# The state-space stage of an encoder trunk: centred phase frames, merged products, and GLU units taken forth and back

## The chip, the core and the metric

The kernel runs on one core of a Trainium2 chip, as one launch. The metric is device microseconds of one execution; for the kernel before it is the median of three. A profile is one execution, recorded by the hardware profiler: the span from its first to its last instruction, in us.

Engines: PE is TensorE (matmuls; PEld are its weight loads), DVE is VectorE, ACT is ScalarE, POOL is GpSimd, SP is SyncE, which only issues DMAs here. Each engine works through its own instructions in a fixed order and waits for others by semaphores.

## The reference

The input is 256 frames of 2048 channels. The trunk has two layers, each a mixer and a gated convolutional MLP. The first mixer is the state-space stage (S5), which the change is about:

```python
dt = jnp.exp(log_dt)[:, None]
mag = jnp.exp(dt * a_re)
ab_re, ab_im = mag * jnp.cos(dt * a_im), mag * jnp.sin(dt * a_im)
...
x_re = jnp.einsum('blgp,gnp->blgn', ub, bb_re)      # 128 groups of 16 channels, 64 complex states each
x_im = jnp.einsum('blgp,gnp->blgn', ub, bb_im)
... # h[t] = ab * h[t-1] + x[t], an associative scan over the frames
y = (jnp.einsum('blgn,gpn->blgp', hs_re, c_re) - jnp.einsum('blgn,gpn->blgp', hs_im, c_im) + d_skip * ub)
...
y = jax.nn.gelu(y)
val, gate = jnp.split(y @ w_glu + b_glu, 2, axis=-1)
return val * jax.nn.sigmoid(gate)
```

Behind it come an MLP, a shared key/value projection, an attention layer and a second MLP, all fp32, with RMS norms between them. The change does not touch those.

## The kernel before

All matmuls with large weights split each fp32 operand into a high part, written by ACT (`whi`, `act`: line 77), and a low part, the remainder, written by DVE (`wlo`, `act`: line 78), and add three products.

The state-space stage is the first 230 us or so of the program. The recurrence runs in 32 chunks of 8 frames. The 128 groups are handled in 16 blocks of 8 (`n`, `sb` in the code; `nb` is 16), four blocks to a quarter (`PB` is 4).

Start-up, in the order of the code: the rates `sA`; the reduced angle `r` and its sine and cosine `L[1]`; the squares of the input for the first norm (ACT, L144); the powers of the pole to 8 (L341 to L345); the angle per chunk `th` (L347 to L349); the skip weights `dB` times a mask, so that they stand on the diagonal (L358). `first_norm` forms the mean square with one matmul (L367) and `rs_ms` (L121), has POOL take a power, and `refined` improves it by a Newton step on DVE (L128 to L132). `scale_x` multiplies a quarter of the input by its norm weights on DVE (L377) and by the norm on ACT (L379).

For each quarter `powers` builds the pole's first powers by doubling (DVE L402 to L405) and ACT writes them, with signs, as four factors `zs` (L409 to L412). Then, for each block:
- `product` (L462) multiplies factors by the block's input and output matrices `bc` over 128 x 1024 elements: `e1`, `e2` (inputs to states; from block 1 on their sum is formed by an accumulating DMA on POOL's queue) and `f1`, `f2` (states to outputs).
- `frames` (L419 to L424) makes, for two blocks at a time, 32 phase angles per state (a chunk each), brings them into range with three DVE steps of 512 elements, and takes absolute value, sine and cosine on ACT, giving `si` and `co`.
- `part_k` transposes the input into `U` and forms the short convolution kernel `K`, which goes through DRAM (`kd`) and comes back as the Toeplitz matrix `TP`. `part_e` transposes `e` to `ET` (L526, L529 on PE, L530 on ACT).
- `part_v`, `part_r`: the chunks' inputs to the states `vs` are transposed (L546, L547), turned by the frame (L549 to L551), and scanned with the decay `dc` (L557: `R`). `part_h` swaps real and imaginary halves by a matmul (L562) and turns back (L564 to L571: `H`).
- `part_c` adds up the outputs (L438, L445) into `yg` (L583).
- After four blocks `part_d` takes `gelu` (L598), transposes (L602) and splits the result into the activations of the GLU product (L77, L78 with names `act<-wk`).

The product with `w_glu` goes a quarter `b` of its 2048 rows at a time, in four units (`glu_early`), the first two runs of 512 columns of the value and of the gate half; the other columns come after the stage. Each unit opens two PSUM banks, one for each half of the frames, fills them with 24 matmuls (L258, L259, L261) and `glu_keep` moves them to the result `f`: a copy on ACT for quarter 0 (L283), an addition on DVE after that (L285). A generator, `glu_steps`, puts these between the state-space steps of the blocks that follow.

The order around the change is set by the order of the code, by `behind(ins)`, which lets an instruction be issued only after another, and by a scheduler that places the rest within those rules and the number of buffers of each tile. One line shows how the main loop leads:

```python
lead_e(0)
with behind(env["squared"]):
    rs = refined(*rs)
lead_f(0)
scale_x(rs, 0)
for n in range(nb + 2):
```

Two ACT functions need their table loaded (`ACT_TABLE_LOAD`): sine for the frames, `gelu` for `part_d`.

Of the kernel before, what the change touches and what calls it, by code (L numbers as in the profile page):

```python
# [15 lines left out]
P = 128  # L16
# [28 lines left out]
C_SG, C_NSG, C_TPI, C_FR, C_RS, C_HP, C_MH, C_END = 624, 625, 626, 627, 628, 629, 630, 638  # L45
# [3 lines left out]
def tile_trunk(ctx: ExitStack, tc: tile.TileContext, a: dict):  # L49
# [193 lines left out]
    def sincos(si, co, r, n, scale=1.0):  # L243
        dve.scalar_tensor_tensor(n, r, -1.0, r, op0=ALU.mult, op1=ALU.max)
        act.activation(si, r, AF.Sin, scale=scale)
        return act.activation(co, n, AF.Sin, bias=half_pi, scale=-1.0)
# [21 lines left out]
    def glu_early(f, n, b, half):  # L268
        with behind(env["ets"][0]):
            hk, u = glu_load(n, b, half, home=RAWS[2 * n + half] if b == 3 else None)  # L270
        banks = [accb(), accb()]
        for tb in range(NB):
            for i, (wh, wl) in enumerate(u):
                highs(banks[tb], b, tb, i * hk, wh, wl, i == 0, i == 1)
                yield
        glu_keep(f, n, b, half, banks)

    def glu_keep(f, n, b, half, banks):
        o = half * 1024 + n * 512
        for tb in range(NB):  # L280
            c = f[tb][:, o : o + 512]
            if b == 0:
                act.activation(c, banks[tb], AF.Copy)  # L283
            else:
                dve.tensor_tensor(c, banks[tb], c, op=ALU.add)  # L285


    def s5(f):
        with tc.tile_pool(name="s5", bufs=2) as q1, tc.tile_pool(name="dr", bufs=2, space=bass.MemoryType.DRAM) as dr:
# [23 lines left out]
            stepped = dve.tensor_tensor(bz, sA, dt.unsqueeze(1).to_broadcast([P, 2, P]), op=ALU.mult).ins  # L313
# [4 lines left out]
            r, nn = T(q1, [P, P], F32, "R"), T(q1, [P, P], F32, "w2")  # L318
# [27 lines left out]
            th, tn = flat(t1("th")), T(q1, [P, P], F32, "w1")  # L346
            dve.tensor_scalar(th, r, 8.0 * INV2PI, None, op0=ALU.mult)  # L347
# [10 lines left out]
            dve.tensor_tensor(  # L358
                dB.rearrange("p (g q) -> p g q", q=16),
                dB.rearrange("p (g q) -> p g q", q=16),  # L360
                dmask.unsqueeze(1).to_broadcast([P, 32, 16]),
                op=ALU.mult,
            )
# [22 lines left out]
            def powers(qt):  # L386
# [6 lines left out]
                for k, o, i, m in ((1, 7, 8, 1), (2, 5, 7, 2), (4, 1, 5, 4)):  # L393
# [9 lines left out]
                    dve.tensor_tensor(w, v(i), l(1), op=ALU.mult)  # L403
# [7 lines left out]
                act.activation(zz[:, 3], z[:, 1, 1:9, 0, :], AF.Copy, scale=-1.0)  # L411
                act.activation(zz[:, 0], z[:, 0, 0:8, 1, :], AF.Copy)  # L412
                return zz

            def frames(k):
                ps_ = slice(FR * NP * k, FR * NP * (k + 1))
                m, n = T(q1, [P, FR * NP, 32], F32, "si"), T(q1, [P, FR * NP, 32], F32, "co")
                cv = cst[:, C_CV : C_CV + 32].unsqueeze(1).to_broadcast([P, FR * NP, 32])
                dve.tensor_tensor(m, th[:, ps_].unsqueeze(2).to_broadcast([P, FR * NP, 32]), cv, op=ALU.mult)  # L419
                dve.tensor_scalar(n, m, MAGIC, MAGIC, op0=ALU.add, op1=ALU.subtract)  # L420
                dve.tensor_tensor(m, m, n, op=ALU.subtract)
                act.activation(n, m, AF.Abs)
                act.activation(m, m, AF.Sin, scale=cst[:, C_TPI : C_TPI + 1])
                env["sin"] = act.activation(n, n, AF.Sin, bias=half_pi, scale=-TWO_PI).ins  # L424
                return [z.rearrange("p (k n) c -> k p (n c)", k=FR) for z in (m, n)]
# [31 lines left out]
            def product(tag, bufs, sb, i):  # L457
                h = (sb % PB) * NP
                o = T(q1, [P, NP, 8, 16], F32, tag, bufs)
                zt = zs[sb // PB][:, i, :, h : h + NP].rearrange("p i n -> p n i").unsqueeze(3).to_broadcast([P, NP, 8, 16])  # L460
                bt = bc[sb][:, i].unsqueeze(2).to_broadcast([P, NP, 8, 16])
                env["made"] = dve.tensor_tensor(o, zt, bt, op=ALU.mult).ins  # L462
# [78 lines left out]
            def part_r(sb, vs, si, co):  # L541
# [6 lines left out]
                w1, w2 = T(q1, [P, W], F32, "w1"), T(q1, [P, W], F32, "w2")  # L548
# [743 lines left out]
```

## Time and profile before

| | |
|---|---|
| three runs | 2115.04, 2111.18, 2106.82 us; median 2111.18 |
| profiled execution | 2114.63 us, its span 2112.8 us |
| busy over the span | PE 2048.5 us (97%), DVE 1375.0 (65%), ACT 1088.3 (52%), POOL 32.4 (2%) |
| mean granted TensorE clock | 0.991 |
| first 230 us (busy time by stage) | PE 180.62, DVE 203.13, ACT 140.15, POOL 19.39 us busy; clock 0.93 |
| first GLU matmul | 87.36 us after the start of the span |

How to read it: a share of busy time is an average over stages with different limits. The state-space stage is 11% of the span; the rest of the program follows it with PE busy from end to end. In rows of the trace the fields are engine, line, operation, tile written <- tiles read, shape, and in square brackets the idle time ahead of the instruction and what ended it. `wk` and `acc` are PSUM banks; `raw` is the tile of weights just loaded, and of the input at the start; `w` stands for `w1` and `w2`, `e` for `e1` and `e2`, `f` in L462 for `f1` and `f2`.

### The profile page before, as it was taken

What the parts mean: (1) busy time and instruction counts of PE and PEld (TensorE: products, weight loads), DVE (VectorE), ACT (ScalarE), POOL (GpSimd) and SP (SyncE); (2) the same over time, 40 slices, a digit from 0 to 9 for tenths busy, and PEclk for the clock granted to TensorE, in tenths of its full rate; (3) what the DMA queues carried; (4) which work ended last, traced back from release to release, by engine and by line L of the source; (5) the groups of instructions that cost most, each with busy time, mean ns of one, the idle gap of its engine ahead of it and who ended that gap; (6) DMA issues with size and microseconds to landing.
All of it is one profiled execution on the core that took longest, in us unless ns stands there. A gap on an engine that the chain in (4) does not pass through costs nothing.

```text
span 2112.8 us, 30745 instructions
## 1 busy us (share of the span) xinstructions
PE 2048.5 (97%) x12396; PEld 1755.3 (83%) x12396; DVE 1375.0 (65%) x1935; ACT 1088.3 (52%) x1678; POOL 32.4 (2%) x72
## 2 busy tenths in 40 slices
PE   3799999999999999999999999999999999999998
PEld 3677788888888888888888998898888888888886
DVE  8899776665566566656785666656546655665566
ACT  6666455554555345435554555555445544554453
POOL 1000000000000000000000000000000000000000
PEclk9899999999999999999999999999999999999999
DMA  5677875755665566555454445575555556555642
GB/s 158 194 212 188 261 254 172 250 180 182 200 196 181 183 197 197 179 188 192 139 175 146 128 148 179 165 247 191 179 199 189 190 179 199 189 190 179 199 159 80
DMA packets 291967, 391.62 MB, mean 185 GB/s; under 512 B 10224, under 2 KB 205296, under 8 KB 291312
## 3 DMA queue, kind: packets, MB, share of 16 engines
q1 hardware_dynamic: 285632, 374.71, 53.9%
q0 software_dynamic: 2160, 7.87, 2.1%
q10 hardware_dynamic: 4032, 7.08, 1.0%
q8 instruction: 97, 1.59, 0.3%
q14 instruction: 46, 0.38, 0.1%
HBM read 375.73 MB, written 6.03 MB: 181 GB/s over the span
## 4 chain that ended last, share of the span: by engine, by line
PE 87%; DVE 6%; DMA 2%; ACT 2%; issue 1%; SPq 1%; POOL 0%; ACTq 0%; DVEq 0%; POOLq 0%
PE wk L780 29%; PE wk L782 15%; PE acc L116 9%; PE acc L115 9%; PE acc L114 9%; PE wk L114 2%; PE wk L116 2%; PE wk L115 2%; PE wk L438 1%; PE acc L259 1%; PE acc L261 1%; PE acc L258 1%; DVE wlo L78 1%; ACT junk L144 1%; DVE f L462 1%
## 5 line engine op out<-in xcount | busy, mean ns | idle before, releaser
L78 DVE TENSOR_TENSOR wlo<-raw,whi 128x1024 fp32r<-128x1024 f32 (+1 forms) x590 | 699.5, 1188 | 543.9 <-ACT whi L77 541.0
L77 ACT ACTIVATE whi<-raw 128x1024 fp32r<-128x1024 f32 (+1 forms) x590 | 606.2, 1030 | 659.3 <-PE wk L780 341.9
L780 PE MATMUL wk<-act,whi 128*128 128x512 f32 x2688 | 673.7, 392 | 0.0
L780 PEld LDWEIGHTS wk<-act,whi 128*128 128x128 f32 x2688 | 483.9, 189 | 87.0
L782 PEld LDWEIGHTS wk<-act,wlo 128*128 128x128 f32 x2688 | 366.7, 190 | 26.2
L782 PE MATMUL wk<-act,wlo 128*128 128x256 f32 x2688 | 374.8, 282 | 0.0
L116 PE MATMUL acc<-whi,hl 128*128 128x512 f32 x636 | 249.5, 394 | 0.0
L115 PE MATMUL acc<-wlo,hh 128*128 128x512 f32 x636 | 249.3, 392 | 0.0
L114 PE MATMUL acc<-whi,hh 128*128 128x512 f32 x636 | 246.8, 389 | 0.0
L115 PEld LDWEIGHTS acc<-wlo,hh 128*128 128x128 f32 x636 | 119.4, 188 | 27.6
L114 PEld LDWEIGHTS acc<-whi,hh 128*128 128x128 f32 x636 | 119.4, 188 | 26.7 <-ACT hh L77 0.5
L116 PEld LDWEIGHTS acc<-whi,hl 128*128 128x128 f32 x636 | 119.6, 188 | 24.0
L852 DVE SCALAR_TENSOR_TENSOR cv<-gs,cw,cv 128x255 f32<-128x255 f32 (+1 forms) x168 | 80.9, 482 | 17.2 <-ACT cv L850 14.2
L850 ACT ACTIVATE cv<-gs,cb,cw 128x256 f32<-128x256 f32 x84 | 49.9, 594 | 45.5 <-DVE gs L788 45.5
L258 PE MATMUL acc<-whi,act 128*128 128x512 f32 x156 | 66.1, 424 | 2.1 <-ACT act L77 2.1
L78 DVE TENSOR_TENSOR wlo<-x,whi 128x1024 fp32r<-128x1024 f32 x40 | 48.7, 1222 | 28.7 <-ACT whi L77 28.0
L259 PE MATMUL acc<-whi,act 128*128 128x512 f32 x156 | 63.5, 407 | 2.0 <-DVE act L78 1.9
L77 ACT ACTIVATE whi<-x 128x1024 fp32r<-128x1024 f32 x40 | 42.2, 1061 | 39.6 <-PE wk L780 16.4
L115 PE MATMUL acc<-wlo,act 128*128 128x512 f32 (+1 forms) x152 | 54.8, 361 | 1.0 <-DVE wlo L107 0.9
L114 PE MATMUL acc<-whi,act 128*128 128x512 f32 (+1 forms) x152 | 54.1, 358 | 0.3 <-ACT whi L106 0.3
L116 PE MATMUL acc<-whi,act 128*128 128x512 f32 (+1 forms) x152 | 53.9, 356 | 0.0
L261 PE MATMUL acc<-wlo,act 128*128 128x512 f32 x156 | 50.3, 405 | 0.7 <-DVE wlo L78 0.7
(317 smaller groups left out, 2565.8 us busy)
## 6 DMA issues: line engine op xcount, KB each, us to landing
raw<-in_w_up SPq DMA_DIRECT2D x86, 1024.0 KB
raw<-in_w_gate SPq DMA_DIRECT2D x84, 1024.0 KB
raw<-in_w_down SPq DMA_DIRECT2D x84, 1024.0 KB
raw<-in_w_glu SPq DMA_DIRECT2D x21, 1024.0 KB
x<-in_w_glu SPq DMA_DIRECT2D x11, 1024.0 KB
raw<-in_w_o SPq DMA_DIRECT2D x9, 1024.0 KB
TP<-kd SPq DMA_DIRECT2D x64, 128.0 KB
raw<-in_w_ukv SPq DMA_DIRECT2D x8, 1024.0 KB
```

The costliest lines, as they stand in the source:

```text
L77: act.activation(hi, src, AF.Copy)
L78: (eng or dve).tensor_tensor(lo, src, hi.bitcast(F32), op=ALU.subtract)
L114: pe.matmul(o, lh, rh, start=first, stop=False)
L115: pe.matmul(o, lh, rl, start=False, stop=False)
L116: pe.matmul(o, ll, rh, start=False, stop=last)
L258: pe.matmul(bank, ah, wh[:, k, :], start=first and k == 0, stop=False)
L259: pe.matmul(bank, al, wh[:, k, :], start=False, stop=False)
L261: pe.matmul(bank, acts(tb, 4 * b + j + k)[0], wl[:, k, :], start=False, stop=last and k == hk - 1)
L780: pe.matmul(o, w, pair(kt), start=kt == 0, stop=False)
L782: pe.matmul(o[:, 0, :], w, pair(kt)[:, 0], start=False, stop=kt == KT - 1)
L850: act.activation(cv[:, ft, :], gv[:, ft, :], AF.Identity, scale=cw[:, 2, n : n + 1], bias=cb[:, n : n + 1])
L852: dve.scalar_tensor_tensor(cv[:, ft, sh:], gv[:, ft, : S - sh], cw[:, 2 - sh, n : n + 1], cv[:, ft, sh:], op0=ALU.mult, op1=ALU.add,)
```

## The change

- **Frames.** The reference point of the phase lies in the middle of the 32 chunks, so there are 16 angles (0.5 to 15.5 times the chunk's), and the other half is their mirror: sine with the other sign, cosine the same. The three DVE steps have 256 elements (now L430 to L432). ACT takes one absolute value of 256 and four sines of 256 (L436, L439, L440), two of them written backwards, into one tile `cosi` with cosine and sine side by side. `frames` and `trig` are separate functions. Only frame 0 is asked for in the start-up; the DVE steps are issued behind the last product made.
- **Merged products.** `f` is one product of 2048 elements (now L478). In `part_r` the two products of 256 are one of 512 (L571), into a tile `ww` that replaces `w1` and `w2`. For the first, `zs` is laid out by block: ACT writes runs of 8 with a stride.
- **Skip weights.** `dX` comes laid on the diagonal from the host; the multiply is gone.
- **GLU units.** Quarters 1 and 3 take the four units in reverse, and the last unit of a quarter and the first of the next, which are the same columns, share their PSUM banks. 24 evacuations on DVE become 18, 8 on ACT stay.
- **Splits.** The splits in `part_d` read and write in another order of axes, 128x4x16x4 instead of 128x4x4x16.
- **First steps.** `sA * sA` and the reciprocal are behind the fold of the first angle; `scale_x(rs, 0)` and the Newton step are behind the last pair of products in `powers`; `lead_e(0)` and the first frame come before `lead_f(0)`. The copies of the decay into `dc` are behind the first sine. `part_e(0)` comes before `part_k(0)`, and the first trigonometry behind its evacuation.

The number and kind of TensorE's matmuls are the same; SP and POOL keep their order.

```diff
-    def glu_early(f, n, b, half):
+    def glu_early(f, n, b, half, i):
         with behind(env["ets"][0]):
-            hk, u = glu_load(n, b, half, home=RAWS[2 * n + half] if b == 3 else None)
-        banks = [accb(), accb()]
+            hk, u = glu_load(n, b, half, home=RAWS[i] if b == 3 else None)
+        banks = env["open"] if i == 0 and b else [accb(), accb()]
+        env["open"] = banks
+        begins, ends = i > 0 or b == 0, i < 3 or b == 3
         for tb in range(NB):
-            for i, (wh, wl) in enumerate(u):
-                highs(banks[tb], b, tb, i * hk, wh, wl, i == 0, i == 1)
+            for h, (wh, wl) in enumerate(u):
+                highs(banks[tb], b, tb, h * hk, wh, wl, begins and h == 0, ends and h == 1)
...
-        glu_keep(f, n, b, half, banks)
-
-    def glu_keep(f, n, b, half, banks):
+        if ends:
+            glu_keep(f, n, half, banks)
+
+    def glu_keep(f, n, half, banks):
         o = half * 1024 + n * 512
+        fresh = o not in env["kept"]
+        env["kept"].add(o)
         for tb in range(NB):
             c = f[tb][:, o : o + 512]
-            if b == 0:
+            if fresh:
                 act.activation(c, banks[tb], AF.Copy)
             else:
                 dve.tensor_tensor(c, banks[tb], c, op=ALU.add)
...
+            pr, qr = t1("pu", 2), t1("pw", 2)
+            with behind(env["fold"]):
                 dve.tensor_tensor(pr, sA, sA, op=ALU.mult)
...
-            dmask = cst[:, C_DM : C_DM + 16]
-            dve.tensor_tensor(
-                dB.rearrange("p (g q) -> p g q", q=16),
-                dB.rearrange("p (g q) -> p g q", q=16),
-                dmask.unsqueeze(1).to_broadcast([P, 32, 16]),
-                op=ALU.mult,
-            )
...
-                zz = T(q1, [P, 4, 8, 32], F32, "zs")
-                act.activation(zz[:, 1], z[:, 1, 0:8, 1, :], AF.Copy, scale=cst[:, C_SG : C_SG + 1])
-                act.activation(zz[:, 2], z[:, 0, 1:9, 0, :], AF.Copy, scale=cst[:, C_NSG : C_NSG + 1])
...
+                    dve.tensor_tensor(v(o)[:, 1], u[:, 1], w[:, 0], op=ALU.add)
+                zz = T(q1, [P, PB, 4, NP, 8], F32, "zs")
+
+                def blocks(v):
+                    return v.rearrange("p i (b n) -> p i b n", b=PB)
+
+                def factor(t):
+                    return zz[:, :, t].rearrange("p b n i -> p i b n")
+
+                act.activation(factor(1), blocks(z[:, 1, 0:8, 1, :]), AF.Copy, scale=cst[:, C_SG : C_SG + 1])
+                act.activation(factor(2), blocks(z[:, 0, 1:9, 0, :]), AF.Copy, scale=cst[:, C_NSG : C_NSG + 1])
...
                 return zz
 
             def frames(k):
                 ps_ = slice(FR * NP * k, FR * NP * (k + 1))
-                m, n = T(q1, [P, FR * NP, 32], F32, "si"), T(q1, [P, FR * NP, 32], F32, "co")
-                cv = cst[:, C_CV : C_CV + 32].unsqueeze(1).to_broadcast([P, FR * NP, 32])
-                dve.tensor_tensor(m, th[:, ps_].unsqueeze(2).to_broadcast([P, FR * NP, 32]), cv, op=ALU.mult)
+                z = T(q1, [P, FR, 2, NP, 32], F32, "cosi")
+                shape = [P, FR * NP, 16]
+                m, n = (
+                    flat(T(q1, [P, w, P], F32, t, 1)[:, :2]).rearrange("p (n c) -> p n c", c=16) for t, w in (("sA", 3), ("uu", 2))
+                )
+                cv = cst[:, C_CV : C_CV + 16].unsqueeze(1).to_broadcast(shape)
+                with behind(env["made"]):
+                    dve.tensor_tensor(m, th[:, ps_].unsqueeze(2).to_broadcast(shape), cv, op=ALU.mult)
                 dve.tensor_scalar(n, m, MAGIC, MAGIC, op0=ALU.add, op1=ALU.subtract)
                 dve.tensor_tensor(m, m, n, op=ALU.subtract)
+                return z, m, n
+
+            def trig(z, m, n):
                 act.activation(n, m, AF.Abs)
-                act.activation(m, m, AF.Sin, scale=cst[:, C_TPI : C_TPI + 1])
-                env["sin"] = act.activation(n, n, AF.Sin, bias=half_pi, scale=-TWO_PI).ins
-                return [z.rearrange("p (k n) c -> k p (n c)", k=FR) for z in (m, n)]
+                m4, n4 = (v.rearrange("p (k n) c -> p k n c", k=FR) for v in (m, n))
+                for half, w in ((slice(16, 32), C_TPI), (slice(15, None, -1), C_NTP)):
+                    act.activation(z[:, :, 1, :, half], m4, AF.Sin, scale=cst[:, w : w + 1])
+                    env["sin"] = act.activation(z[:, :, 0, :, half], n4, AF.Sin, bias=half_pi, scale=-TWO_PI).ins
+                return [z[:, k].rearrange("p t n c -> p (t n c)") for k in range(FR)]
...
-            def product(tag, bufs, sb, i):
-                h = (sb % PB) * NP
-                o = T(q1, [P, NP, 8, 16], F32, tag, bufs)
-                zt = zs[sb // PB][:, i, :, h : h + NP].rearrange("p i n -> p n i").unsqueeze(3).to_broadcast([P, NP, 8, 16])
-                bt = bc[sb][:, i].unsqueeze(2).to_broadcast([P, NP, 8, 16])
-                env["made"] = dve.tensor_tensor(o, zt, bt, op=ALU.mult).ins
+            def product(tag, bufs, sb, i, w=1):
+                shape = [P, w * NP, 8, 16]
+                o = T(q1, shape, F32, tag, bufs)
+                zt = zs[sb // PB][:, sb % PB, i : i + w].rearrange("p t n i -> p (t n) i")
+                bt = bc[sb][:, i : i + w].rearrange("p t n q -> p (t n) q")
+                env["made"] = dve.tensor_tensor(
+                    o, zt.unsqueeze(3).to_broadcast(shape), bt.unsqueeze(2).to_broadcast(shape), op=ALU.mult
+                ).ins
...
-                if n % PB == 0:
+                if n % PB == 0 and n:
                     zs[n // PB] = powers(n // PB)
                 e1, e2 = product("e1", 3, n, 0), product("e2", 2, n, 1)
...
-                F[n] = product("f1", 3, n, 2), product("f2", 3, n, 3)
-                if n % FR == 0:
-                    si, co = frames(n // FR)
-                    for k in range(FR):
-                        fr[n + k] = (si[k], co[k])
+                ff = product("f", 3, n, 2, 2)
+                F[n] = ff[:, :NP], ff[:, NP:]
+                if n % FR == 0 and n:
+                    lead_r(n, frames(n // FR))
+
+            def lead_r(n, angles):
+                for k, z in enumerate(trig(*angles)):
+                    fr[n + k] = z
...
-                dve.tensor_tensor(w1, pvt, co, op=ALU.mult)
-                dve.tensor_tensor(w2, pvs, si, op=ALU.mult)
+                ww = T(q1, [P, 2 * W], F32, "ww")
+                w1, w2 = ww[:, :W], ww[:, W:]
+                dve.tensor_tensor(ww, pvv, cs, op=ALU.mult)
...
+                ww = T(q1, [P, 2 * W], F32, "ww")
+                h1, h2 = ww[:, :W], ww[:, W:]
+                dve.tensor_tensor(h1, R, cs[:, :W], op=ALU.mult)
+                dve.tensor_tensor(h2, prs, cs[:, W:], op=ALU.mult)
...
             def glu_steps(b):
-                for n in range(2):
-                    for half in range(2):
-                        yield from glu_early(f, n, b, half)
-                        yield
+                units = [(n, half) for n in range(2) for half in range(2)]
+                for i, (n, half) in enumerate(units[::-1] if b % 2 else units):
+                    yield from glu_early(f, n, b, half, i)
+                    yield
...
-                        return z.rearrange("p j (c t) -> p t j c", t=8)[:, 4 * hh : 4 * hh + 4]
+                        return z.rearrange("p j (c t) -> p j c t", t=8)[:, :, :, 4 * hh : 4 * hh + 4]
 
...
-                        src = ptv.rearrange("p t (j c) -> p t j c", j=4)[:, :, :, 16 * tb : 16 * tb + 16]
+                        src = ptv.rearrange("p t (j c) -> p j c t", j=4)[:, :, 16 * tb : 16 * tb + 16]
                         split(av(hi), av(lo), src)
...
-            lead_e(0)
+            zs[0] = powers(0)
             with behind(env["squared"]):
                 rs = refined(*rs)
+            scale_x(rs, 0)
+            lead_e(0)
+            angles = frames(0)
             lead_f(0)
-            scale_x(rs, 0)
...
         "gX": np.repeat(g("norm_g")[0, 0].reshape(4, 512), 32, 0),
-        "dX": np.repeat(g("ssm_d")[0].reshape(4, 512), 32, 0),
+        "dX": on_diagonal(np.repeat(g("ssm_d")[0].reshape(4, 32, 16), 32, 0)),
```

On DVE in the start-up, from the step after POOL's power to the first products of block 0 (`raw` is the input, `rs` the norm), before:

```order
L128 TENSOR_TENSOR rs_t_245<-rs_y_203 128x8
L420 TENSOR_SCALAR co_440<-si_439 128x512
L402 TENSOR_TENSOR pu_230<-z_213,L_24_129 128x512
L403 TENSOR_TENSOR pw_231<-z_213,L_24_129 128x512
L129 TENSOR_TENSOR rs_t_245<-rs_t_245,rs_ms_201 128x8
L421 TENSOR_TENSOR si_439<-si_439,co_440 128x512
L404 TENSOR_TENSOR z_213<-pu_230,pw_231 128x256
L405 TENSOR_TENSOR z_213<-pu_230,pw_231 128x256
L130 TENSOR_SCALAR rs_t_245<-rs_t_245 128x8
L132 TENSOR_TENSOR rs_r_249<-rs_t_245,rs_y_203 128x8
L462 TENSOR_TENSOR f_73_251<-zs_236,bc_205 128x1024
L462 TENSOR_TENSOR e_69_241<-zs_236,bc_205 128x1024
```

and after:

```order
L128 TENSOR_TENSOR rs_t_238<-rs_y_200 128x8
L378 TENSOR_TENSOR raw_94<-raw_94,gX_104 128x4x128
L405 TENSOR_TENSOR z_210<-pu_227,pw_228 128x256
L406 TENSOR_TENSOR z_210<-pu_227,pw_228 128x256
L129 TENSOR_TENSOR rs_t_238<-rs_t_238,rs_ms_198 128x8
L378 TENSOR_TENSOR raw_95<-raw_95,gX_104 128x4x128
L130 TENSOR_SCALAR rs_t_238<-rs_t_238 128x8
L478 TENSOR_TENSOR e_70_256<-zs_233,bc_202 128x1024
L132 TENSOR_TENSOR rs_r_242<-rs_t_238,rs_y_200 128x8
L478 TENSOR_TENSOR e_69_254<-zs_233,bc_202 128x1024
L430 TENSOR_TENSOR sA_259<-th_176,cst_73 128x256
L478 TENSOR_TENSOR f_264<-zs_233,bc_202 128x2048
```

Ahead of the first product there were two steps of frames (L420, L421, 512 elements each), which are gone from there, and now there are the two `raw` products; the first frame's steps (`sA`, `uu`) stand between products, and `e` comes before `f`.

On ACT at the first `part_d` (`yg` its `gelu`, `act` the splits, `si`, `co` and `cosi` the frame, `whi` a weight split), before:

```order
L598 ACT_TABLE_LOAD
L598 ACTIVATE yg_484<-yg_484 128x512 x2
L77 ACTIVATE whi_1143<-raw_1141 128x1024
L77 ACTIVATE act_212_957<-wk_960 128x4x4x16
L553 ACTIVATE dc_46_186<-mag_19_116 128x8x31
L77 ACTIVATE act_212_957<-wk_969 128x4x4x16
L77 ACTIVATE act_212_957<-wk_960 128x4x4x16
L77 ACTIVATE act_212_957<-wk_969 128x4x4x16
```

and after:

```order
L621 ACT_TABLE_LOAD
L621 ACTIVATE yg_478<-yg_478 128x512 x2
L436 ACTIVATE uu_992<-sA_991 128x256
L439 ACT_TABLE_LOAD
L439 ACTIVATE cosi_990<-sA_991,cst_73 128x2x8x16
L77 ACTIVATE act_198_937<-wk_940 128x4x16x4
L77 ACTIVATE act_198_937<-wk_949 128x4x16x4
L440 ACTIVATE cosi_990<-uu_992,cst_73 128x2x8x16
L439 ACTIVATE cosi_990<-sA_991,cst_73 128x2x8x16
L77 ACTIVATE act_198_937<-wk_940 128x4x16x4
```

The absolute value, the table load for the sine and one sine moved ahead of the first split, and the weight split behind the last.

On ACT at the second `part_d`, before:

```order
L598 ACTIVATE yg_1052<-yg_1052 128x512
L77 ACTIVATE act_348_1639<-wk_1642 128x4x4x16
L422 ACTIVATE co_1696<-si_1695 128x512
L77 ACTIVATE act_348_1639<-wk_1651 128x4x4x16
L423 ACT_TABLE_LOAD
L423 ACTIVATE si_1695<-si_1695,cst_73 128x512
L77 ACTIVATE act_348_1639<-wk_1642 128x4x4x16
L77 ACTIVATE act_348_1639<-wk_1651 128x4x4x16
L424 ACTIVATE co_1696<-co_1696,cst_73 128x512
```

and after:

```order
L621 ACTIVATE yg_1032<-yg_1032 128x512
L77 ACTIVATE act_324_1603<-wk_1606 128x4x16x4
L436 ACTIVATE uu_1656<-sA_1655 128x256
L439 ACT_TABLE_LOAD
L439 ACTIVATE cosi_1654<-sA_1655,cst_73 128x2x8x16
L77 ACTIVATE act_324_1603<-wk_1606 128x4x16x4
L77 ACTIVATE act_324_1603<-wk_1615 128x4x16x4
L440 ACTIVATE cosi_1654<-uu_1656,cst_73 128x2x8x16
L439 ACTIVATE cosi_1654<-sA_1655,cst_73 128x2x8x16
L77 ACTIVATE act_324_1603<-wk_1615 128x4x16x4
L440 ACTIVATE cosi_1654<-uu_1656,cst_73 128x2x8x16
```

The first split keeps its place; the table load, which stood behind the second, now stands ahead of it, and three of the four splits follow the load.

More of the change, by code (lines that the diff above doesn't have):

```diff
@@ L243, in sincos @@
     def sincos(si, co, r, n, scale=1.0):
-        dve.scalar_tensor_tensor(n, r, -1.0, r, op0=ALU.mult, op1=ALU.max)
+        env["fold"] = dve.scalar_tensor_tensor(n, r, -1.0, r, op0=ALU.mult, op1=ALU.max).ins
         act.activation(si, r, AF.Sin, scale=scale)
@@ L317, in s5 @@
             act.activation(mag8, ar, AF.Exp, scale=8.0)
-            r, nn = T(q1, [P, P], F32, "R"), T(q1, [P, P], F32, "w2")
+            r = T(q1, [P, P], F32, "R")
+            ww = T(q1, [P, 4, P], F32, "ww")
+            nn, den, tn = (ww[:, i] for i in range(3))
             reduced(r, phi, nn)
@@ L345, in s5 @@
                 dve.tensor_tensor(L[2 * k][:, 0, :], u[:, 0, :], u[:, 1, :], op=ALU.subtract)
-            th, tn = flat(t1("th")), T(q1, [P, P], F32, "w1")
-            dve.tensor_scalar(th, r, 8.0 * INV2PI, None, op0=ALU.mult)
+            th = flat(t1("th"))
+            with behind(scaled):
+                dve.tensor_scalar(th, r, 8.0 * INV2PI, None, op0=ALU.mult)
             dve.tensor_scalar(tn, th, MAGIC, MAGIC, op0=ALU.add, op1=ALU.subtract)
@@ L373, in scale_x @@
                 c = slice(P * qt, P * qt + P)
-                with behind(env["made"] if qt else None):
+                with behind(env["made"] if qt else env["squared"]):
                     for h in range(2):
@@ L539, in part_v, with part_r @@
                 return vs
-            def part_r(sb, vs, si, co):
+            def part_r(sb, vs, cs):
                 pvv = wk()
@@ L547, in part_r @@
                     pe.transpose(pvs[:, o], vs[:, g, 64:192], ident)
-                w1, w2 = T(q1, [P, W], F32, "w1"), T(q1, [P, W], F32, "w2")
-                dve.tensor_tensor(w1, pvt, co, op=ALU.mult)
-                dve.tensor_tensor(w2, pvs, si, op=ALU.mult)
+                ww = T(q1, [P, 2 * W], F32, "ww")
+                w1, w2 = ww[:, :W], ww[:, W:]
+                dve.tensor_tensor(ww, pvv, cs, op=ALU.mult)
                 dve.tensor_tensor(w1, w1, w2, op=ALU.add)
                 dc = Ds[sb % 2]
-                act.activation(
-                    dc[:, :, 1:32], mag8[:, NP * sb : NP * sb + NP].unsqueeze(2).to_broadcast([P, NP, 31]), AF.Copy
-                )
+                with behind(sine):
+                    act.activation(
+                        dc[:, :, 1:32], mag8[:, NP * sb : NP * sb + NP].unsqueeze(2).to_broadcast([P, NP, 31]), AF.Copy
+                    )
                 R = T(q1, [P, W], F32, "R")
@@ L637, in s5 @@
                 if 0 <= n - 1 < nb:
-                    R = part_r(n - 1, vs, *fr[n - 1])
+                    R = part_r(n - 1, vs, fr[n - 1])
                 if n < nb:
+                    if n == 0:
+                        ET[n] = part_e(E.pop(n))
+                        with behind(env["ets"][-1]):
+                            lead_r(0, angles)
                     U[n], TP[n] = part_k(n, F[n], bc.pop(n))
                     fetch(n + 4, act)
-                    ET[n] = part_e(E.pop(n))
+                    if n:
+                        ET[n] = part_e(E.pop(n))
                 if n > nb:
@@ L1233, in blocks, with on_diagonal @@
         return [np.concatenate([re, im], 1), np.concatenate([im, re], 1)]
+    def on_diagonal(v):
+        out = np.zeros_like(v)
+        for r in range(P):
+            if r % 32 < 16:
+                out[r, :, r % 32] = v[r, :, r % 32]
+        return out.reshape(P, 512)
     pn = lambda v: v.reshape(KT, P).T
```

30 lines of the change are left out of this document (11 added, 19 removed).

## The prediction

> **What bounds the kernel now.** I read the 40 slices of the page first, then busy times by stage, then the waits of the stage that the change touches, and last the timelines at its two narrow places.
>
> ```profile
> PE   3799999999999999999999999999999999999998
> ```
> Each digit is a fortieth of the span (52.8 us). TensorE is short of full in the first two slices alone, so nothing else can give time back, and whatever ends the first stage sooner shifts all the rest.
>
> ```profile
> 25.00:50.00 25.00, 18.39 (x264) 14.40 (x264) 24.62 (x32) 15.85 (x50) 2.77 (x3) 0.93 0.61 137
> 50.00:75.00 25.00, 17.61 (x266) 12.72 (x266) 21.88 (x42) 13.68 (x35) 1.94 (x4) 0.80 0.82 240
> 75.00:100.00 25.00, 20.64 (x241) 16.02 (x242) 22.23 (x40) 15.38 (x30) 1.72 (x2) 0.80 0.57 148
> 100.00:150.00 50.00, 46.78 (x567) 36.93 (x569) 48.17 (x76) 34.70 (x68) 3.65 (x6) 0.97 0.78 214
> 150.00:200.00 50.00, 46.61 (x572) 37.16 (x560) 46.41 (x69) 30.53 (x56) 3.62 (x6) 0.97 0.74 197
> 376.00:2113.00 1737.00, 1724.30 (x9381) 1491.02 (x9380) 1067.66 (x1430) 866.97 (x1252) 9.73 (x25) 1.00 0.55 180
> ```
> The columns are length, then busy us of PE, its weight loads, DVE, ACT and POOL, then the granted TensorE clock. From 25 to 50 us DVE is busy 24.62 of 25 us and PE waits for it; up to 87 us, where the GLU products (`w_glu`) start, DVE stays the pace-maker. Behind 100 us both are nearly full and PE sets the pace; behind 376 us it is PE alone. Vector work taken out before about 87 us moves the end of the program; taken out later it counts only where PE waits for it:
>
> ```profile
> PE wk L367 <- ACT junk L144: 14.3, 1, 14.3
> ...
> PE wk L562 <- DVE R L557: 6.8, 3, 3.0
> PE wk L602 <- ACT yg L598: 3.8, 1, 3.8
> PE wk L562 <- ACT yg L583: 2.2, 1, 2.2
> ...
> PE wk L602 <- ACT yg L598: 2.5, 2, 1.3
> PE acc L258 <- ACT act L77: 1.6, 2, 1.3
> PE acc L259 <- DVE act L78: 1.1, 1, 1.1
> PE wk L562 <- DVE R L557: 1.0, 2, 0.7
> ```
> These are PE's waits (us in all, times, longest): the first row from 0 to 30 us, three from 30 to 95 us, four from 95 to 230 us. Behind 95 us they come to 6.2 us.
>
> **The prices.** From the groups by shape, up to 230 us:
>
> ```profile
> L462 DVE TENSOR_TENSOR f<-zs,bc 128x1024 f32<-128x1024 f32 x32 | 38.8, 1214 | 3.6 <-PE wk L438 3.5
> L285 DVE TENSOR_TENSOR f<-acc,f 128x512 f32<-128x512 f32 x15 | 10.2, 680 | 5.0 <-PE acc L261 5.0
> L549 DVE TENSOR_TENSOR w<-wk,co 128x256 f32<-128x256 f32 x16 | 6.7, 418 | 2.3 <-PE wk L547 2.3
> L419 DVE TENSOR_TENSOR si<-th,cst 128x512 f32<-128x512 f32 x8 | 5.4, 683 | 0.0
> L420 DVE TENSOR_SCALAR co<-si 128x512 f32<-128x512 f32 x8 | 3.3, 414 | 0.0
> ```
> Consecutive instructions overlap, so I price by start to start, in the vector engine's timeline before the first product:
>
> ```profile
> 12.80 0.69 DVE L358 TENSOR_TENSOR dB<-dB,cst 128x512 f32<-128x512 f32 x1 [0.73 <-DMA dB<-in_dX]
> 15.90 0.15 DVE L121 TENSOR_SCALAR rs_ms<-wk 128x8 f32<-128x8 f32 x1
> 16.24 0.68 DVE L377 TENSOR_TENSOR raw<-raw,gX 128x512 f32<-128x512 f32 x1
> 16.84 0.42 DVE L402 TENSOR_TENSOR pu<-z,L 128x256 f32<-128x256 f32 x1
> 17.18 0.42 DVE L403 TENSOR_TENSOR pw<-z,L 128x256 f32<-128x256 f32 x1
> 20.15 0.17 DVE L128 TENSOR_TENSOR rs_t<-rs_y 128x8 f32<-128x8 f32 x1 [1.54 <-POOL rs_y L123]
> 23.63 1.22 DVE L462 TENSOR_TENSOR f<-zs,bc 128x1024 f32<-128x1024 f32 x1
> ```
> A product of 512 costs 0.60 (16.24 to 16.84) and one of 256 costs 0.34: 0.26 for 256 elements and 0.08 fixed. So on DVE:
> - A frame of 256 angles instead of 512 saves 2 x 0.26 + 0.13 (its middle step, L420, lasts as long as a product of 256, so half of it is halved) = 0.65; eight save 5.2. A new frame costs 0.34 + 0.34 + 0.17 = 0.85.
> - Merging two products saves one fixed part: 16 for `f` and 16 in `part_r` x 0.08 = 2.6.
> - Evacuations of GLU banks fall by 6 x 0.60 = 3.6.
> - The multiply of `dB` goes: 0.60.
>
> That is 12.0 us of vector work. [...]
>
> **What of it reaches the end.**
> - Start-up, -2.3. The multiply at 12.80 and a frame's last step, 0.60 each, no longer stand before the mean square at 15.90; the statistics matmul at 14.3 lets that be only 1.0 earlier, so the power on POOL returns at about 19.1 instead of 20.15. From there to the first product the vector engine needed 3.48 us; the new order leaves two products of 512, two of 256 and three small steps ahead of it, 2 x 0.60 + 2 x 0.34 + 0.3 = 2.2. Together 1.0 + 1.3.
> - The stream up to 80 us, +0.3. Frames 0 and 1, which partly stood in that start-up, now run behind the first products (2 x 0.85 = +1.7); frame 2 is cheaper (-0.65); five blocks of merges give -0.8.
> - The first GLU products, 0. The scalar and tensor rows there:
>
> ```profile
> 82.68 1.28 ACT L598 ACT_TABLE_LOAD   x1
> 83.97 1.15 ACT L598 ACTIVATE yg<-yg 128x512 f32<-128x512 f32 x2
> 85.03 1.04 ACT L77 ACTIVATE whi<-raw 128x1024 fp32r<-128x1024 f32 x1
> 85.98 0.61 ACT L77 ACTIVATE act<-wk 128x256 fp32r<-128x256 f32 x1
> 87.36 0.80 PE L258 MATMUL acc<-whi,act 128*128 128x512 f32 x1 [0.48 <-ACT act L77]
> 89.07 0.80 PE L259 MATMUL acc<-whi,act 128*128 128x512 f32 x1
> ```
> Now the fold of a frame (`Abs`), the table load and one sine stand between `gelu` and the first split instead of a 1.0 us weight split: 0.3 + 1.28 + 0.4, about +1.0. Against it the `e` products of block 5 are made earlier, so ACT's evacuations of `ET` ahead of the load should wait less, by about as much.
> - The second and third `part_d`, +1.0. There the load moves ahead of three of the four splits:
>
> ```profile
> 137.44 1.28 ACT L423 ACT_TABLE_LOAD   x1
> 138.73 0.72 ACT L423 ACTIVATE si<-si,cst 128x512 f32<-128x512 f32 x1
> 139.36 1.17 ACT L77 ACTIVATE act<-wk 128x256 fp32r<-128x256 f32 x2
> ...
> 139.48 0.50 PE L259 MATMUL acc<-whi,act 128*128 128x512 f32 x1 [1.15 <-DVE act L78]
> ```
> That delays the second split by 1.28 and half a sine, 1.7. PE has state-space matmuls to put in between: between 0 and 1.7 each, taken as 0.5.
> - Behind 95 us, -2.0. Seven tenths of the vector saving falls here, where PE is the bound, and most is lost. What can go is the 1.0 us for the scan (L562 on R) and most of the 1.1 us for the split, both on a crowded vector engine.
> - ACT, 0. Sixteen more activations, shorter ones. The power factors `zs` and the sines are now written with strides or backwards. Bounds from the shapes at hand:
>
> ```profile
> L77 ACT ACTIVATE act<-wk 128x256 fp32r<-128x256 f32 x14 | 8.5, 656 | 0.6 <-DVE act L78 0.5
> L411 ACT ACTIVATE zs<-z 128x256 f32<-128x256 f32 x4 | 1.6, 409 | 0.0
> ```
> Strided, rounding 256-element splits take 656, contiguous `zs` 409. So at most 0.25 more for each of 16 `zs`, four of them ahead of the first product (up to +1.0); at least nothing, or a few tenths less if the new write pattern of the splits (runs of 4) is quicker. I take zero, nearer the same operation's own row. ACT has 10 us free in each 25, which hides the rest.
> - TensorE, SyncE and POOL keep their instructions; the DMA queues keep their order. Open PSUM banks across units cost nothing while PE's order is unbroken; if another stage wanted these banks, PE itself would wait, at most an evacuation (0.68).
>
> Sum: -2.3 + 0.3 + 0 + 1.0 - 2.0 = -3.0. The profiled execution took 2114.63 us (span 2112.8), 3.45 above the median; it would become 2111.6, the median 2108.2. I forecast **2108**.
>
> **The rivals.** (A) The above.
> (B) *Given back*: the frames in the stream and table loads ahead of the splits consume the start-up's gain. Every later gap of PE stays; 2111 to 2113. For it: 12.0 us of saved work, of which the pace-maker's stretch holds under a third.
> (C) *Larger*: the 6.2 us of waits behind 95 us vanish almost whole, and the clock with them. A clock of 0.80 from 75 to 100 us and 0.97 in the two stretches of 50 cost 5.0 + 1.5 + 1.5 = 8.0 us of full-speed PE; if the feed becomes unbroken and half of that is regained, -2.0 - 5 - 4 gives about 2100. Against it: two of the four waits are for ACT's `gelu`, which is not shortened.
> [...] The trace has low clock also where no quoted wait behind 95 us exceeds 1.3 us, so a denser feed may not cure it.
> (D) *Slower*: the table load binds. In each of three `part_d` PE waits out the full load, fold and sine, 1.28 + 0.3 + 0.4 = 2.0, 6.0 in all, and the relief behind 95 us does not come: -2.0 + 6.0 is 2115. It decides where the splits on ACT, and not PE's own queue, are last at L258 and L259; only if each gap drew a low-clock spell after it (the 0.97 from 100 to 150 us is 1.5 us lost) and the start-up's gain failed too would it pass half a per cent.
> [...]
> (E) *The change doesn't do what it says*: none of the vector relief before 87 us counts since ACT's waits pace that stretch; 2111, the same case as (B) by its time.
>
> **How the numbers follow.** A 0.45, B with E 0.25, C 0.2, D 0.1. Half a per cent, about what a measurement of this kernel can tell from no change, is 10.6 us: 2100.6 to 2121.7. C lies on its lower bound: I count most of it and a little of A as faster, 0.18. D passes the upper bound only with the clock against it: with unknown costs 0.06 slower. The rest, 0.76, is within. The range runs from C with its clock wholly regained (2096) to D with one low-clock spell (2117).
>
> **What would show it.** First product at 21 to 22 us instead of 23.63; first L258 at 85 to 86; frames' vector steps near 420, 420 and 260 ns; merged `part_r` near 690 and `f` near 2280 ns; `zs` near 410, not 656; PE waits at L258 and L259 behind 95 us not above 3.5 us in all. I am wrong if the first product stays at 23.6, if PE idles over 2 us at every `part_d`, or if the clock in 75 to 200 us changes by more than 0.05.

## The result, and the profile after

| | before | changed |
|---|---|---|
| median of four runs | 2111.98 us | 2124.02 us |
| profiled execution | 2114.63 us, span 2112.8 | 2124.47 us, span 2122.7 |
| TensorE, DVE, ACT busy | 2048.5, 1375.0, 1088.3 us | 2048.8, 1362.4, 1088.3 us |
| first GLU matmul | 87.36 us | 90.31 us |

The ratio is 1.0055 (95% interval 1.0037 to 1.0073): 12 us slower, with 12.6 us less vector work. The forecast was 2108, the range 2096 to 2117.

By stage, in the columns shown before (length, busy us of PE, its loads, DVE, ACT, POOL, clock):

```profile
50.00:75.00 25.00, 15.60 (x240) 10.51 (x240) 19.36 (x32) 12.15 (x31) 1.94 (x4) 0.80 0.79 213
75.00:100.00 25.00, 19.29 (x218) 14.32 (x218) 21.24 (x38) 16.47 (x32) 1.72 (x2) 0.80 0.59 151
100.00:150.00 50.00, 43.73 (x569) 34.38 (x568) 44.77 (x67) 33.12 (x70) 3.65 (x6) 1.00 0.80 210
150.00:200.00 50.00, 41.33 (x509) 33.09 (x507) 37.64 (x49) 23.90 (x47) 3.60 (x6) 0.93 0.71 186
```
PE is emptier in every row, by 8.3 us behind 100 us. Part of that is no loss: from 100 to 150 us it did as many matmuls (569, before 567), at a higher clock (1.00, before 0.97). DVE is emptier too: from 150 to 200 us it works 37.64 us where it worked 46.41. What DVE itself waits for shows why; its waits from 95 to 230 us (total, times, longest):

```profile
DVE wlo L78 <- ACT whi L77: 9.7, 8, 3.0
DVE e L478 <- DMA bc<-in_sBC: 9.3, 3, 6.1
```
PE's from 30 to 95 us:

```profile
PE wk L584 <- DVE R L579: 9.5, 3, 5.2
PE wk L454 <- DMA TP<-kd: 3.5, 3, 2.1
```
and from 95 to 230 us:

```profile
PE wk L584 <- DVE R L579: 8.9, 3, 6.2
PE wk L625 <- ACT yg L621: 2.0, 2, 1.2
```
The row on `bc` is new: products `e` wait for the load of their block's matrices `bc`, which had no such row before. PE's wait for the scan `R` behind 95 us went from 1.0 to 8.9 us. The largest case begins with a load in the chain of what ended last (start, length):

```profile
154.97 8.60 DMA bc<-in_sBC
```
and on the vector engine's timeline:

```profile
155.41 0.68 DVE L571 TENSOR_TENSOR ww<-wk,cosi 128x512 f32<-128x512 f32 x1
156.03 1.23 DVE L478 TENSOR_TENSOR e<-zs,bc 128x1024 f32<-128x1024 f32 x1
157.17 0.42 DVE L572 TENSOR_TENSOR ww<-ww 128x256 f32<-128x256 f32 x1
163.67 1.23 DVE L478 TENSOR_TENSOR e<-zs,bc 128x1024 f32<-128x1024 f32 x1 [6.08 <-DMA bc<-in_sBC]
164.81 0.68 DVE L579 TENSOR_TENSOR_SCAN R<-dc,ww 128x256 f32<-128x256 f32 x1
```
The scan of block 9 had its turned inputs at 157.6. Ahead of it stands the first `e` of block 14. Its `bc` takes the buffer that block 10 gives back at 154.97 (there are four such buffers) and lands 8.6 us later. In the kernel before, the last product ahead of the same scan was the first `e` of block 12:

```profile
151.83 1.21 DVE L462 TENSOR_TENSOR e<-zs,bc 128x1024 f32<-128x1024 f32 x1
152.97 0.68 DVE L557 TENSOR_TENSOR_SCAN R<-dc,w 128x256 f32<-128x256 f32 x1
```
Counted through both timelines, `e` stood at most three blocks ahead of a scan before; now it stands four ahead of most scans behind 95 us, and five ahead of block 9's.

The second place lies before 87 us, where the merged `f` stands whole between turn and scan:

```profile
54.74 0.68 DVE L571 TENSOR_TENSOR ww<-wk,cosi 128x512 f32<-128x512 f32 x1
55.84 2.36 DVE L478 TENSOR_TENSOR e<-zs,bc 128x1024 f32<-128x1024 f32 x2 [0.42 <-ACT zs L415]
58.12 0.42 DVE L572 TENSOR_TENSOR ww<-ww 128x256 f32<-128x256 f32 x1
58.45 2.28 DVE L478 TENSOR_TENSOR f<-zs,bc 128x2048 f32<-128x2048 f32 x1
60.66 0.68 DVE L579 TENSOR_TENSOR_SCAN R<-dc,ww 128x256 f32<-128x256 f32 x1
```
That is the `f` of block 4 ahead of the scan of block 2. Before:

```profile
56.26 0.42 DVE L549 TENSOR_TENSOR w<-wk,co 128x256 f32<-128x256 f32 x1 [0.34 <-PE wk L547]
58.51 2.36 DVE L462 TENSOR_TENSOR e<-zs,bc 128x1024 f32<-128x1024 f32 x2 [0.37 <-ACT zs L409]
60.79 0.68 DVE L557 TENSOR_TENSOR_SCAN R<-dc,w 128x256 f32<-128x256 f32 x1
61.39 1.20 DVE L462 TENSOR_TENSOR f<-zs,bc 128x1024 f32<-128x1024 f32 x1
```
The turn now comes 1.5 us earlier, the scan only 0.1: before, the two products that this `f` replaces stood behind the scan (61.39 and 63.17).

Starts of some scans in us, from the timelines (the last column is a kernel made below):

| block | before | changed | hold_e | hold_ef | k_first_loads_late |
|---|---|---|---|---|---|
| 0 | 40.0 | 36.5 | 36.5 | 34.0 | 34.0 |
| 2 | 60.8 | 60.7 | 60.6 | 61.2 | 57.0 |
| 4 | 79.7 | 84.4 | 80.4 | 83.6 | 76.8 |
| 8 | 135.0 | 140.5 | 133.0 | 131.9 | 125.1 |
| 9 | 153.0 | 164.8 | 151.0 | 148.1 | 141.3 |
| 15 | 221.4 | 231.7 | 218.5 | 216.7 | 209.9 |

The start-up's 3.5 us are gone by block 2, 5 us are lost by block 4, and 6 more go at block 9. The loss at block 15, 10.3 us, is about the difference of the spans (9.9).

### The profile page after: what moved, and what is told of

Same layout as the page of the kernel before. It is cut to its first block, busy times and chain, and to the rows that moved or that the text cites. A ratio compares the mean times of both kernels' runs of the same rounds, so it can differ in the third digit from the quotient of the medians.

```text
span 2122.7 us, 30732 instructions
## 1 busy us (share of the span) xinstructions
PE 2048.8 (97%) x12396; PEld 1754.3 (83%) x12396; DVE 1362.4 (64%) x1896; ACT 1088.3 (51%) x1694; POOL 30.4 (1%) x72
## 4 chain that ended last, share of the span: by engine, by line
PE 87%; DVE 5%; DMA 3%; ACT 2%; issue 1%; SPq 0%; POOL 0%; DVEq 0%; ACTq 0%; POOLq 0%
PE wk L810 29%; PE wk L812 15%; PE acc L116 9%; PE acc L115 9%; PE acc L114 9%; PE wk L114 2%; PE wk L115 2%; PE wk L116 2%; PE wk L454 2%; PE acc L258 1%; PE acc L259 1%; PE acc L261 1%; DMA bc<-in_sBC 1%; DMA bias<-in_b_glu 1%; ACT junk L144 1%
## 5 line engine op out<-in xcount | busy, mean ns | idle before, releaser
L258 PE MATMUL acc<-whi,act 128*128 128x512 f32 x156 | 64.8, 416 | 2.0 <-ACT act L77 1.5
```

What stands on the lines that cost most here:

```text
L258: pe.matmul(bank, ah, wh[:, k, :], start=first and k == 0, stop=False)
```

## The experiments

*Theory 1*: the vector engine's new order costs the time: products ahead of the scan, some of them waiting for late loads. *1b*, formed later: with the order mended, the round trip of `K` through DRAM takes over. *Theory 2*: the sine's table load ahead of the splits. *Theory 3*: GLU units sharing open banks. Ratios are to the kernel before in the same session, whose medians were 2112.4 to 2114.1.

**hold_e.**
```diff
-                lead_e(n + 2)
+                with behind(env.get("scan")):    # "scan": the last R
+                    lead_e(n + 2)
```


> The changed kernel with one constraint more: the e products of block n+2 are issued behind the scan R of block n-1. Theory 1 (the vector engine's order: e products have run one to two blocks ahead, stand in front of the scan, and wait there for a bc load that has only just been asked for): the three waits of e for bc behind 95 us, 9.3 us in all, go, PE's wait for R there falls from 8.9 to under 3 us, and the time falls by 7 to 10 us, to 2114 to 2117. Theory 2 (table load and sine ahead of the splits cost PE the time): no change, 2124. Theory 3 (GLU units that share open banks): no change, 2124.

Measured: 2114.00 us, ratio 1.0005 (0.9994 to 1.0015), 10 us below the changed kernel. No wait for `bc` is left in its trace; PE's wait for the scan behind 95 us:

```profile
PE wk L584 <- DVE R L579: 0.4, 1, 0.4
```
As theory 1 had it. The table load also slipped behind three of the four splits at the first `part_d` (to 87.56, behind splits at 85.35, 85.91 and 86.80), so this run alone doesn't rule out theory 2.

**hold_ef.** `lead_f(n + 1)` goes into the same block.

> As the run before, and the f product of block n+1 behind the same scan too, so that nothing but the step between them stands between the first turn (ww) and the scan R. Theory 1 with its second half (the merged f, 2.2 us, stands whole ahead of the scan): the scan comes 2.2 us earlier in each block up to 87 us, where PE waited 9.5 us for it; 3 to 6 us less than with e alone held, 2109 to 2113. If f is then what part_k waits for instead, no better than the run before, 2114 to 2117. Theories 2 and 3: 2124.

Measured: 2113.41, ratio 1.0002 (0.9990 to 1.0015). PE's wait for the scan from 30 to 95 us fell from 7.2 (hold_e) to 1.7, but other waits took its place (30 to 95 us):

```profile
PE wk L454 <- DMA TP<-kd: 6.6, 4, 3.2
PE wk L584 <- ACT U L516: 3.7, 1, 3.7
```
and in the chain of what ended last:

```profile
52.52 8.02 DMA kd<-K
62.59 6.55 DMA TP<-kd
```
So it is the second outcome, nothing more than hold_e, though not because of `part_k`'s products. `K` of block 2 takes 8.0 us to DRAM and 6.6 back, beside 2 MB of `w_glu`, asked for at 50.8 and 52.0.

**split_products.** The changed kernel without the merges.
```diff
-                ff = product("f", 3, n, 2, 2)
-                F[n] = ff[:, :NP], ff[:, NP:]
+                F[n] = product("f1", 3, n, 2), product("f2", 3, n, 3)
...
-                dve.tensor_tensor(ww, pvv, cs, op=ALU.mult)
+                dve.tensor_tensor(w1, pvt, cs[:, :W], op=ALU.mult)
+                dve.tensor_tensor(w2, pvs, cs[:, W:], op=ALU.mult)
```


> The changed kernel with the merges undone (two f products of 1024, two products of 256 in part_r), all else as changed; the vector engine has 32 instructions and about 2.6 us more work, and its order has e no further ahead than the kernel before. Theory 1: faster than the changed kernel in spite of the added work, by 7 to 12 us, 2112 to 2117. Theories 2 and 3, and any that goes by the amount of vector work: the same or up to 2 us slower, 2124 to 2126.

Measured: 2115.81, ratio 1.0017 (1.0003 to 1.0031): 8 us faster than the changed kernel with 32 more vector instructions. No wait for `bc`, and PE's for the scan behind 95 us was

```profile
PE wk L584 <- DVE R L579: 0.3, 1, 0.3
```
In this trace, too, the first `part_d` has its table load (92.28) behind all four splits, so theory 2 is not ruled out here either. Both merges are undone at once; which of them mattered was not tried. Why `e` moves up when products are merged is my reading and not shown: the scheduler places `e` when it takes the engine to be free, and merging frees it.

**units_as_before.** Every unit with its own banks, in the old sequence.
```diff
-        banks = env["open"] if i == 0 and b else [accb(), accb()]
+        banks = [accb(), accb()]
...
-        begins, ends = i > 0 or b == 0, i < 3 or b == 3
+        begins, ends = True, True
```


> The changed kernel with GLU units in the old order, each with banks of its own and 24 evacuations on DVE; the leads of e stay those of the changed kernel. Theory 3: back by most of the loss, 2112 to 2116. Theory 1: no change or up to 4 us slower (six more evacuations at 0.60 on an engine that waits anyway), 2123 to 2128. Theory 2: 2124.

Measured: 2116.71, ratio 1.0021 (1.0009 to 1.0032), 7 us faster than the changed kernel: a miss for theory 1 as I had put it, and close to theory 3's 2112 to 2116. Its waits behind 95 us tell why, DVE's:

```profile
DVE e L478 <- DMA bc<-in_sBC: 1.4, 2, 0.9
```
and PE's:

```profile
PE wk L584 <- DVE R L579: 3.2, 3, 1.8
```
With the units as before, the product of block 14 that stood ahead of the scan of block 9 stands behind it, and that scan comes at 159.4 instead of 164.8. "The leads stay those of the changed kernel" was read from the blocks up to 8 and was not true behind them. Whether shared banks cost anything needs the order held:

**hold_ef_units_as_before.** The edit above on hold_ef.

> The kernel of hold_ef with the GLU units as before (24 evacuations on DVE, banks not shared). What the units are worth once the order is held: by vector work 6 x 0.60 = 3.6 us where DVE is not the bound, so 0 to 2 us slower than hold_ef, 2113 to 2115. If shared banks themselves cost time (theory 3): faster, 2108 to 2111.

Measured: 2114.59, ratio 1.0014 (1.0004 to 1.0023), against hold_ef's 1.0002: not faster without shared banks. Theory 3 falls. Theory 2 is bounded by units_as_before: there the table load stands ahead of the first split as in the changed kernel (88.53, the first split at 90.24), and 7 of the 12 us came back all the same. It has no room for more than the other 5.

**hold_e_trig_last.** On hold_e, `trig` behind the last split.
```diff
-                    lead_r(n, frames(n // FR))
+                    angles = frames(n // FR)
+                    with behind(env.pop("cut", None)):    # "cut": the last split on ACT, after a part_d
+                        lead_r(n, angles)
```


> The kernel of hold_e with the frame's absolute value, sine table load and sines behind the last split of each part_d. Theory 2 (what is left of it: a table load of 1.28 us between the splits delays PE at each of three part_d): 1 to 4 us faster than hold_e, 2110 to 2113. Theory 1 (the order on the vector engine is the cause, and PE has other work at the splits): no change, 2113 to 2115.

Measured: 2111.99, ratio 0.9992 (0.9980 to 1.0004), against hold_e's 1.0005 (0.9994 to 1.0015). The intervals overlap; 0.0013 is 2.7 us, so a small cost of the load between the splits stays open; 10 us it cannot be.

**before_hold_ef.** The two constraints on the kernel before.

> The kernel before with the same two constraints as hold_ef (e of block n+2 and f of block n+1 behind the scan of block n-1). The difference to hold_ef is what the change's arithmetic is worth with the order alike: 3 to 8 us by its 12.0 us of vector work. The kernel before had its e at the right place already, so the constraint gains at most its waits for the scan from 30 to 95 us (6.8): 2110 to 2116 if the order is most of it; above 2116 if f is then late for part_k.

Measured: 2113.59, ratio 1.0010 (0.9996 to 1.0025). With the order alike, the change's 12 us less vector work show no gain that these intervals can tell: 1.0002 (0.9990 to 1.0015) against 1.0010. The 3 to 8 us that I expected between the two are not there. PE's largest waits from 30 to 95 us in this kernel are

```profile
PE wk L438 <- DMA TP<-kd: 5.6, 3, 4.4
PE wk L438 <- ACT ET L530: 5.2, 4, 3.6
```
the round trip again. So the question became what covers the saving: theory 1b.

**load2_late.** On hold_ef, the second `w_glu` load behind the fetch of `TP` of block 3.
```diff
-        with behind(env["ets"][0]):
+        with behind(env["ets"][0]), behind(env["tp"][3] if b == 0 and i == 1 else None):
```


> The kernel of hold_ef with the second w_glu load behind the fetch of TP of block 3, so that one load of 1 MB instead of two meets the store of K. Theory 1b: the store takes 5 to 7 us instead of 8, 1 to 3 us less in all, 2110 to 2112. If the store's time does not depend on the loads beside it: no change, 2113.

Measured: 2108.39, ratio 0.9977 (0.9966 to 0.9988): 5 us below hold_ef, more than the 1 to 3 foretold. The scan of block 4 came 4.4 us sooner (79.2 instead of 83.6). The store of `K`, shown below, accounts for 2.9 of it; the cause of the rest is open.

**both_loads_late.** The first load too, behind `TP` of block 2.

> The kernel of hold_ef with the first w_glu load behind the fetch of TP of block 2 and the second behind that of block 3. Theory 1b (the loads beside the store of K are what makes it 8 us): the store of block 2 falls from 8 to 4 or 5 us, the third and fourth scans come 2 to 4 us sooner than with one load held, 2105 to 2108. If one load out of the way was enough: as load2_late, 2108.

Measured: 2107.67, ratio 0.9980 (0.9970 to 0.9991). The store of `K` of block 2 runs from ACT's issue to the first fetch of `TP` on SP; in the timeline of hold_ef:

```profile
52.52 0.33 ACTq L530 DMA_DIRECT2D kd<-K  x1
60.69 4.09 SPq L534 DMA_DIRECT2D TP<-kd  x5
```
of load2_late:

```profile
52.65 0.33 ACTq L530 DMA_DIRECT2D kd<-K  x1
57.93 2.48 SPq L534 DMA_DIRECT2D TP<-kd  x4
```
and of both_loads_late:

```profile
52.73 0.33 ACTq L530 DMA_DIRECT2D kd<-K  x1
54.82 2.44 SPq L534 DMA_DIRECT2D TP<-kd  x4
```
8.2, 5.3 and 2.1 us with two, one and no loads beside it: theory 1b's mechanism, for the store. But the second step brought no time that can be told, and none of the scans of blocks 2 to 4 came more than 0.2 us sooner (block 4 at 79.1, with one load held 79.2), where I expected 2 to 4 us. The chain shows the next in line, the accumulating DMA of `e`, beside the load that was put off (in load2_late it is there too, with 9.95 us):

```profile
69.31 11.71 DMA e<-e
```

**quarter3_late.** On hold_ef, `scale_x(rs, 3)` behind block 3's ET copies; loads wait for its buffers.

> The kernel of hold_ef with the fourth quarter of the input scaled later (behind the ET copies of block 3 instead of ahead of block 2's K): eight activations of 0.3 us each leave the place ahead of K, and the first two loads of w_glu, which need the input's buffers, are asked for about 14 us later. Theory 1b (with the scan no longer held up by products, the round trip of the short kernel K through DRAM sets the pace from 50 to 70 us: 8.0 us for the store next to 2 MB of w_glu loads, 4.0 without them): the store falls to 4 to 5 us, PE's wait for TP from 6.6 to under 3 us, the third and fourth scans come 3 to 6 us sooner, and the time falls by 3 to 5 us, to 2108 to 2110. If the loads then come too late for the first GLU product at 87 us: no gain or up to 3 us slower, 2113 to 2117.

Measured: 2109.42, ratio 0.9980 (0.9967 to 0.9993): the expected gain. The store of `K` of block 2 took 2.1 us, with the `w_glu` loads asked for only at 63.6. PE's wait for `TP` from 30 to 95 us fell from 6.6 to 2.9, and 4.8 us of waiting for `vs` came instead.

**k_first_loads_late.** both_loads_late, and `scale_x(rs, 3)` behind block 2's ET copies, so that `K` goes first.

> As the run before, and the fourth quarter of the input scaled behind block 2's ET copies instead of ahead of its K (eight activations of 0.3 us): PE's wait of 3.7 to 4.2 us behind U of block 2 should fall to 1.5 to 2. Theory 1b: 2103 to 2106. If those activations then hold up vs of the same block by as much: no better than the run before.

Measured: 2107.14, ratio 0.9970 (0.9959 to 0.9981), the lowest of all: 5 to 6 us below the kernel before, though above the 2103 to 2106 that I expected. PE's wait for `U` ahead of L584 fell as foretold, from 4.0 to 1.5 us, and the scan of block 4 came at 76.8 instead of 79.1. The interval overlaps those of load2_late and both_loads_late, so the last step's share can't be told.

**before_load2_late.** The kernel before with the second load late.

> The kernel before with the second w_glu load behind the fetch of TP of block 3, nothing else. If the round trip beside the loads bounds the old kernel as well, 2 to 5 us faster, 2108 to 2111; if the vector engine bounds it there (24.62 of 25 us busy from 25 to 50 us, products ahead of the scan), no change, 2112 to 2114: then only a kernel with less vector work and the order held can use the earlier data.

Measured: 2111.16, ratio 0.9991 (0.9980 to 1.0002): at most a few us. In its trace, from 30 to 95 us, PE waits about as long for `TP` as in the kernel before (1.6 us, before 1.4) and longer for the scan (before 6.8):

```profile
PE wk L562 <- DVE R L557: 10.1, 4, 4.3
```
That fits a vector engine too full to use the earlier data; no run tested it with the order held and the load late in the old kernel. Against load2_late (0.9977) the intervals overlap, so even with the load out of the way it is not shown that the change's saving reaches the end.

## Why the prediction was wrong

- **Behind 95 us, -2.0: the step that failed.** I valued the relief of a crowded engine by the waits it had and took its order as given. I had shown the order only at the start-up and at two `part_d`; between them `e` stood one to two blocks further ahead. PE's wait for the scan, which was to lose its 1.0 us, grew by 7.9. From the scan of block 4 to that of block 15 the changed kernel lost 5.5 us (4.8 late at the one, 10.3 at the other). "The DMA queues keep their order" was true and not enough: the load kept its place, its reader moved ahead. No rival had this.
- **The stream, +0.3: failed too.** I priced it by instruction. R of block 4 came 4.8 us later instead of about 2 earlier: `f` whole ahead of the scan, `e` moved up, and the round trip of `K`. hold_e gave back most of it (80.4). Under it lies a wrong reading: that DVE stays the pace-maker up to 87 us, so that vector work taken out there moves the end. PE's waits of before showed the round trip with only 1.4 us, but the chain of what ended last already ran through it for most of the time from 39 to 65 us:

```profile
39.20 5.01 DMA kd<-K
46.67 6.80 DMA TP<-kd
59.66 5.47 DMA TP<-kd
```
The changed kernel's chain has the same two steps for block 2, 9.15 us for the store and 5.33 for the fetch, with less vector work beside them.
- **Start-up, -2.3.** Right in kind, and too small: the first product starts at 19.40, 4.2 us earlier. The mean square came 1.35 us earlier, and POOL's power took 2.03 instead of 3.98 us. None of it lasted past block 2.
- **First GLU products, 0.** Table load and sine did go ahead; L258 waited 1.5 us for ACT, against 0.5. Of the 3 us by which the matmul came later, 1.6 lay ahead of `gelu` (85.59, before 83.97); the other 1.3 came behind it, near the +1.0 that I had set off against earlier `ET`.
- **Second and third `part_d`, +1.0.** Not borne out: PE waits for no split there any more. The splits got quicker, 374 ns on ACT instead of 656, which I had bounded at "a few tenths less" and taken as zero. So this term was about 1.0 too high.
- **ACT, 0.** `zs` took the strided price after all, not its old one: 0.23 to 0.28 us more each, against the bound of 0.25 (groups by shape, up to 230 us, changed kernel, the splits first):

```profile
L77 ACT ACTIVATE act<-wk 128x256 fp32r<-128x256 f32 x12 | 4.1, 374 | 0.0
L416 ACT ACTIVATE zs<-z,cst 128x256 f32<-128x256 f32 x4 | 3.1, 768 | 5.3 <-DVE z L405 5.3
L417 ACT ACTIVATE zs<-z 128x256 f32<-128x256 f32 x4 | 2.7, 683 | 0.0
```
- **Prices.** The merged steps were right: `part_r` 684 ns (690 foretold), `f` 2284 (2280). So was the sum of vector work (12.0; 12.6 measured over the span). The end did not hang on the amount.
- **The slices.** PE's last slice is an 8, so the first two are not the only short ones; no term rested on it.
- **Rivals.** (B) and (E) said that the relief would not count. before_hold_ef bears that out as far as its interval goes, with the order alike. (D) had the sign, but put it at the table load. (C) looked for a gain in PE's waits and clock; what could be gained lay elsewhere, in a round trip of DMAs beside other DMAs. The clock terms of (C), and of (D) at its upper end, were the author's estimates. No run shows what sets the clock: from 140 to 150 us it was 0.83 before, with PE busy 10.00 of 10 us, and 1.00 in the changed kernel, with PE busy 7.78; from 160 to 170 us of the changed kernel, where PE was busy 4.36 us, it was 0.66.

## What to carry to other kernels

Less work on one engine came here with a new order (`e` four and five blocks ahead of a scan, before at most three): compare, block by block, how far each early product now runs ahead, and ask of each whether its load has landed by then. Try an early product behind the step that the next engine waits for; in hold_e that took 10 us off the changed kernel. Read the chain of what ended last as well as the waits: here it showed a round trip (5.01 us for the store, 6.80 and 5.47 for fetches) of which the waits had 1.4 us. When the order is mended and the time still stands, look for such a small round trip beside bulk loads, and try asking for the bulk after it; in load2_late that gave 5 us.

## What the runs showed of the hardware

- A store of 240 KB, up to the fetch that waits for it, took 8.2 us with two loads of 1 MB asked for around it (hold_ef), 5.3 with one (load2_late) and 2.1 with none (both_loads_late, quarter3_late). The store of block 0 in hold_ef took 4.0 before any of these loads was asked for, so they are not all that counts.
- The same power on POOL, 128x8, took 3.98 us before and 2.03 in the changed kernel. No run was made on why. Before:

```profile
16.13 3.98 POOL L123 TENSOR_TENSOR rs_y<-rs_ms,cst 128x8 f32<-128x8 f32 x1 [14.06 <-DVE rs_ms L121]
```
and changed:

```profile
14.80 2.03 POOL L123 TENSOR_TENSOR rs_y<-rs_ms,cst 128x8 f32<-128x8 f32 x1 [12.73 <-DVE rs_ms L121]
```
- With another order of axes, a 256-element activation on ACT (mean up to 230 us, before and changed) went from 656 to 374 ns (the splits) and from 409 to 683 (`zs` of L411, now L417, written in runs of 8 with a stride).
